# Weight sums of the MLPs' first products on GpSimd, and the inner operands prepared in two pairs instead of one

## The chip, the core and the metric

The kernel runs on one core of a Trainium2 chip. The core has engines that run side by side, each through its own queue in order: TensorE (PE) multiplies matrices, VectorE (DVE) and ScalarE (ACT) work element by element, GpSimd (POOL) does so too, and SyncE (SP) issues the transfers (DMAs) between the chip's large memory and the core's on-chip memory. Engines wait for each other by semaphores. The metric is the device time of one execution in microseconds (us); the kernel before takes 1993.26 us (median of 3 runs, 1992.43 to 1994.49).

## What is computed

A network of two layers on 1024 tokens of width 1024, all in float32. Each layer is a mixer (sliding-window attention in the first, a gated linear recurrence called HGRN2 in the second) and an MLP of width 4096:

```python
def sqrelu_mlp(h, w_up, w_down):
    return jnp.square(jax.nn.relu(h @ w_up)) @ w_down
...
    for layer in range(DEPTH):
        h = rmsnorm(x, mix_norm[layer])
        ...                                   # attention or HGRN2
        x = x + y.astype(x.dtype)
        h = rmsnorm(x, mlp_norm[layer])
        x = x + sqrelu_mlp(h, mlp_w_up[layer], mlp_w_down[layer]).astype(x.dtype)
    return rmsnorm(x, final_norm)
```

The change touches `h @ w_up`, the MLP's first product, and, through a shared helper, some of the HGRN2 projections.

## The kernel before

**Precision.** A float32 matrix is split into a high part (`wh` for a weight, a CAST to a narrower float32 form, on ACT or DVE) and a low part (`wl`, the rest, a subtraction on DVE). `mm3` then makes three matrix multiplications (high by high, high by low, low by high), each 128 x 128 weights by 512 columns.

**Strassen.** Each large product is cut into 2 x 2 blocks and made with seven block products instead of eight (the Strassen-Winograd form). They are numbered 1 to 7; products 1, 2 and 4 take raw weights, products 5, 6, 3 and 7 take sums s1, s2, s4 and s3 of raw weights. The operands on the token side are sums too, made once per MLP.

**The first product of an MLP** (`mlp`, which calls `pair`) runs over 16 pairs m = 0 to 15. `pair` calls `strassen_weights`: it loads four raw weight tiles of 128 x 512 (tag `wr`, 6 buffers), makes the four sums (tag `m`, 7 buffers), and splits the weights of the products to come (tags `wh` and `wl`, 5 buffers each). Seven `product` calls follow, five from pair 4 on, 12 multiplications each, and then the ReLU, the square and the sums of the hidden values (tag `t`, 20 buffers), which are stored for the second product. `two`, which makes the projections of HGRN2, calls `strassen_weights` as well, 12 times.

**Inner blocks.** From pair 4 on, products 2 and 4 of a pair are themselves made with seven smaller products of 256 columns, for two pairs at a time. A generator `inner` does this (12 blocks in each MLP, one in each pair from 3 to 14): it loads two raw tiles, makes four sums of 128 x 256, and issues its products between those of the pair. Their token-side operands are made by a generator `prepare(name)`, once for name 2 and once for name 4: it loads four tiles back from the large memory, makes four differences (each as two halves of 128 x 256 on DVE), splits three of them, and stores seven tiles. Both `prepare` generators are stepped between the products of pair AT = 2; in pair 3 `put_in` loads one of the stored tiles of each, splits it and puts it in place.

**The order.** The instructions are not issued in the order of the code. `Schedule` records them all, with a planner's cost for each engine that may do one, and lists them by a simulated clock: PE work keeps about the order of the code, weights are given a lead (`LEAD`), an operation that two engines can do goes to the one that finishes earlier by these costs. `tt` gives the planner's cost of an elementwise operation of two tensors; with the engine `"any"` it goes to DVE. `only(...)` on a tile tells the planner that just a part of it is touched, so that work on another part needn't be ordered against it. The result is one fixed queue for each engine. Nearly all instructions carry the line of the one call in which they are issued, L374 (in `call`), so the profile's rows are told apart by tile names.

Of the kernel before, what the change touches and what calls it, by code (L numbers as in the profile page):

```python
# [15 lines left out]
ALU = mybir.AluOpType  # L16
# [27 lines left out]
LEVELS = 6  # L44
WARM = 10
INNER = (2, 4)
AT = 2
K_SPANS = ((-1, 3), (2, 6), (5, 8))

# [261 lines left out]
def straight(z):  # L311

    return z.rearrange("p (b a) -> p a b", a=2)


def halves(z):

    return z.rearrange("p (a b) -> p a b", a=2)


class Net:
# [88 lines left out]
        self.s.add({e: ways[e] for e in engines}, [out], [in_])  # L410

    def tt(self, e, out, x, y, alu, n=TH):
        cost = {"DVE": 70 + n * 1.04, "Pool": 147 + n * 2.105}
        engines = ("DVE",) if e == "any" else (e,)
        ways = {e: self.call(self.engine(e).tensor_tensor, out, x, y, alu) + (cost[e],) for e in engines}
        self.s.add(ways, [out], [x, y])
# [101 lines left out]
    def rstd(self, acc, inner=1.0, outer=1.0, n=TH):  # L518
        return self.spread(self.token_rstd(acc, inner, outer, n), n)
# [43 lines left out]
    def finish(self, which, r=None):  # L563
# [36 lines left out]
        for j in range(HK):  # L600
            z = stored(j + HK)
            self.tt("any", z, z, t[j], ALU.subtract)
            x[4].append(self.split(z))
            if r is None and 4 in INNER:
                self.quarters[4].append(self.keep(z))
# [28 lines left out]
    def strassen_weights(self, first, second, done=()):  # L634

        self.s.lead = LEAD
        a = {(i, k): self.raw(src[:, k * TH : k * TH + TH]) for i, src in enumerate((first, second)) for k in range(2)}
        s1, s2, s3, s4 = (self.t(tag="m") for _ in range(4))
        self.tt("any", s1, a[1, 0], a[1, 1], ALU.add)
        self.tt("any", s2, s1, a[0, 0], ALU.subtract)  # L640
        self.tt("any", s3, a[0, 0], a[1, 0], ALU.subtract)
        self.tt("any", s4, a[0, 1], s2, ALU.subtract)
        order = ((1, a[0, 0]), (5, s1), (2, a[0, 1]), (6, s2), (3, s4), (7, s3), (4, a[1, 1]))
        w = {name: self.weight_split(z) for name, z in order if name not in done}
        self.s.lead = 0
        return w

    def prepare(self, name):

        near, far = slice(0, TH // 2), slice(TH // 2, TH)  # L650
        u = [self.t() for _ in range(HK)]
        for z, kept in zip(u, self.quarters[name]):
            self.dma(z, kept, 4 * P * TH)
        yield
        made = self.quarters[name] = {}

        def difference(out, x, y):
            for i in range(2):
                self.tt("any", out[:, i].only(i), x(i), y(i), ALU.subtract, TH // 2)

        def stored(k, t):
            made[k] = [self.keep(z.bitcast(F32)) for z in self.split(t.rearrange("p i c -> p (i c)"), self.t)]

        low, high = (lambda c: lambda i: u[i][:, c]), (lambda c: lambda i: u[2 + i][:, c])
        new = lambda: self.t(F32, (P, 2, TH // 2))
        part = lambda t: lambda i: t[:, i].only(i)
        t1 = new()
        difference(t1, low(far), low(near))
        made[5] = self.keep(t1.rearrange("p i c -> p (i c)"))
        yield  # L670
        t2 = new()
        difference(t2, high(far), part(t1))
        stored(6, t2)
        yield
        t3 = new()
        difference(t3, high(far), low(far))
        stored(7, t3)
        yield
        t4 = new()
        difference(t4, high(near), part(t2))  # L680
        stored(4, t4)
        yield
# [13 lines left out]
    def inner(self, name, m, x, y):  # L696

        near, far, half = slice(0, TH // 2), slice(TH // 2, TH), TH // 2
        row, made = {2: 0, 4: 1}[name], self.quarters[name]
        self.s.lead = LEAD  # L700
        a0, a1 = (self.raw(self.io["up"][self.layer, i + row * (MT // 2)][:, TH:]) for i in (m, m + 1))
        sa, sb = self.t(tag="m"), self.t(tag="m")
        s1, s2, s3, s4 = sa[:, near].only(0), sa[:, far].only(1), sb[:, near].only(0), sb[:, far].only(1)
        self.tt("any", s1, a1[:, near], a1[:, far], ALU.add, half)
        self.tt("any", s2, s1, a0[:, near], ALU.subtract, half)
        self.tt("any", s3, a0[:, near], a1[:, near], ALU.subtract, half)
        self.tt("any", s4, a0[:, far], s2, ALU.subtract, half)
        wide = []
        w = {1: (0, near), 2: (0, far), 5: (1, near), 6: (1, far), 7: (2, near), 3: (2, far), 4: (3, far)}
        self.s.lead = 0  # L710
        banks = [self.psum(), self.psum()]
        main, side, own = banks[0][:, near].only(0), banks[1][:, near].only(0), banks[1][:, far].only(1)

        def product(k, ps, start):
            more = {} if start else {"skip_group_check": True}
            n, cols = w[k]
            self.s.lead = LEAD
            if n == 3:
                hi, lo = (self.tile(tag, BUFS[tag], (P, TH), F32R) for tag in ("wh", "wl"))
                self.copy(hi[:, far], a1[:, far], half, ("ACT", "DVE"), False)  # L720
                self.tt("any", lo[:, far], a1[:, far], hi[:, far].bitcast(F32), ALU.subtract, half)
                wide.append((hi, lo))
            elif n == len(wide):
                wide.append(self.weight_split((a0, sa, sb)[n]))
            if k in made:
                right = [self.t(F32R) for _ in range(2)]
                for z, kept in zip(right, made[k]):
                    self.dma(z.bitcast(F32), kept, 4 * P * TH)
            self.s.lead = 0
            for i in range(2):  # L730
                c = slice(cols.start + i * P, cols.start + i * P + P)
                wh, wl = (z[:, c] for z in wide[n])
                if k in made:
                    xh, xl = (z[:, i * half : (i + 1) * half] for z in right)
                else:
                    at = near if k in (1, 2) else far
                    xh, xl = (z[:, at] for z in x[name][i if k in (1, 5) else 2 + i])
                self.mm3(ps, (wh, wl), (xh, xl), start and i == 0, i == 1, half, slice(0, half), **more)

        y.extend(self.t() for _ in range(2))  # L740
        part = {(i, j): y[i][:, (near, far)[j]].only(j) for i in range(2) for j in range(2)}

        def take(z, bank):
            self.copy(halves(z), straight(bank), half)

        def add(z, bank):
            self.tt("DVE", halves(z), straight(bank), halves(z), ALU.add, half)

        product(1, main, True)
        take(part[0, 0], main)  # L750
        yield
        product(2, own, True)
        add(part[0, 0], own)
        yield
        product(6, main, False)
        take(part[0, 1], main)
        yield
        product(5, side, True)
        take(part[1, 1], side)
        yield  # L760
        product(7, main, False)
        add(part[1, 1], main)
        yield
        product(3, side, False)
        add(part[0, 1], side)
        yield
        product(4, main, False)
        take(part[1, 0], main)
        yield
# [56 lines left out]
    def mlp(self, cut):  # L826

        x = self.mlp_second()
        made, n = {}, MT // 2
        for m in range(n):  # L830
            between, first = [], m - m % 2
            if m == AT:
                between += [self.prepare(name) for name in INNER]
            if m == AT + 1:
                between += [self.put_in(name, x[name]) for name in INNER]
            for name in INNER:
                c = first if name == 4 else first + 2
                if AT < c < n and m % 2 == (name == 2):
                    made[name, c] = []
                    between.append(self.inner(name, c, x, made[name, c]))  # L840
            done = {name: made[name, first][m % 2] if name == 2 else lambda: made[4, first][m % 2] for name in INNER if (name, first) in made}
            if m == n - 2:
                self.r = [self.a() for _ in range(NH)]
                for hf in range(NH):
                    self.copy(self.r[hf], self.spread(self.square[hf]))
            if m == 1 and self.layer == 0:
                self.hgrn_constants()
            self.pair(m, x, done, between)
        yield from self.down(cut)
# [881 lines left out]
```

## Time and profile before

| what | value |
|---|---|
| median of 3 runs | 1993.26 us (1992.43 to 1994.49) |
| the profiled execution, its own time | 1992.46 us |
| its span, first to last instruction | 1990.6 us |
| granted TensorE clock | 0.998 |
| ACT busy | 1108.4 us (56%) |

The profile is of one execution. Busy time is time in which at least one instruction of the engine was under way. A row of a group has: line, engine, operation, output <- inputs (tile names without numbers), shape and type, count | busy us, mean ns of one | idle us of the engine just before. A row of the timeline has: start, length, engine, line, operation, tiles, shape, count of merged instructions, and in brackets the idle time before it and what ended it. A matrix multiplication's end is modelled: it is shown as longer than the distance to the next one's start.

### The profile page before, as it was taken

How to read it: one execution, taken by the hardware profiler on the slowest of the kernel's cores; microseconds unless marked ns; L12 is line 12 of the kernel's file. 1: busy time of each engine (PE TensorE's matmuls, PEld its weight loads, DVE VectorE, ACT ScalarE, POOL GpSimd, SP SyncE). 2: the span in 40 equal slices, each digit the busy share in tenths (PEclk: the TensorE clock that was granted, in tenths of full speed). 3: DMA queues.
4: the chain of work that ended last, by engine and by line, in shares of the span. 5: the costliest groups of instructions: out<-in, count | busy, mean ns of one | idle time of the engine just before them, and what ended most of it. 6: DMA issues, size and time to landing. Idle time of an engine off the chain costs nothing.

```text
span 1990.6 us, 34667 instructions
## 1 busy us (share of the span) xinstructions
PE 1968.2 (99%) x11836; PEld 1723.3 (87%) x11836; DVE 1763.1 (89%) x3557; ACT 1108.4 (56%) x2280; POOL 61.9 (3%) x124
## 2 busy tenths in 40 slices
PE   9999999999999999999999999999999999999998
PEld 8877788899998888888888888888889998888887
DVE  8999899898889878899899999989989888987787
ACT  6567797666664423355455555554766666343352
POOL 4030000000000000000000000000000000000001
PEclk9999999999999999999999999999999999999999
DMA  6211464998889977755412212667599888986752
GB/s 224 90 54 59 127 217 162 308 304 290 285 264 319 330 244 244 242 167 179 140 59 81 75 60 86 206 203 253 185 313 305 285 278 280 317 315 211 239 173 85
DMA packets 232401, 411.04 MB, mean 206 GB/s; under 512 B 25504, under 2 KB 35744, under 8 KB 232224
## 3 DMA queue, kind: packets, MB, share of 16 engines
q1 hardware_dynamic: 231648, 408.30, 62.0%
q8 instruction: 93, 1.52, 0.3%
q14 instruction: 84, 0.69, 0.1%
q10 hardware_dynamic: 576, 0.52, 0.1%
HBM read 305.97 MB, written 102.76 MB: 205 GB/s over the span
## 4 chain that ended last, share of the span: by engine, by line
PE 89%; DVE 6%; issue 2%; ACT 2%; DMA 1%; POOL 0%; POOLq 0%; SPq 0%; DVEq 0%; ACTq 0%
PE q L374 51%; PE p L374 39%; DVE t L374 2%; DVE a L374 1%; DVE wl L374 1%; DVE m L374 1%; ACT t L374 1%; ACT a L374 1%; ACT wh L374 0%; ACT m L374 0%; DMA wr<-in_wo 0%; POOL a L374 0%; DMA wr<-in_up 0%; DMA a<-in_x 0%; DMA d<-t 0%
## 5 line engine op out<-in xcount | busy, mean ns | idle before, releaser
L374 PE MATMUL q<-a,wh 128*128 128x512 f32 x2368 | 708.4, 379 | 1.9 <-ACT t L374 1.6
L374 PE MATMUL p<-a,wh 128*128 128x512 f32 (+1 forms) x2304 | 657.7, 365 | 0.9 <-DVE wh L374 0.8
L374 PEld LDWEIGHTS q<-a,wh 128*128 128x128 f32 x2368 | 438.8, 189 | 59.2 <-ACT t L374 2.4
L374 PEld LDWEIGHTS p<-a,wh 128*128 128x128 f32 x2304 | 421.1, 189 | 55.4 <-issue 1.2
L374 PE MATMUL q<-a,wl 128*128 128x512 f32 x1184 | 448.1, 379 | 0.0
L374 PE MATMUL p<-a,wl 128*128 128x512 f32 (+1 forms) x1152 | 418.4, 364 | 0.0
L374 ACT CAST a<-t 128x512 fp32r<-128x512 f32 (+1 forms) x299 | 178.8, 613 | 216.8 <-PE q L374 126.6
L374 DVE TENSOR_TENSOR t<-t,t 128x512 f32<-128x512 f32 (+3 forms) x424 | 256.0, 628 | 11.6 <-ACT t L374 10.3
L374 PEld LDWEIGHTS q<-a,wl 128*128 128x128 f32 x1184 | 223.9, 189 | 30.3
L374 DVE TENSOR_TENSOR wl<-wr,wh 128x512 fp32r<-128x512 f32 (+1 forms) x352 | 233.8, 667 | 12.2 <-ACT wh L374 4.7
L374 PEld LDWEIGHTS p<-a,wl 128*128 128x128 f32 x1152 | 218.2, 190 | 25.1 <-issue 0.4
L374 DVE TENSOR_TENSOR a<-t,a 128x512 fp32r<-128x512 f32 (+2 forms) x334 | 218.4, 677 | 0.5 <-ACT a L374 0.2
L374 DVE TENSOR_TENSOR wl<-m,wh 128x512 fp32r<-128x512 f32 x296 | 201.6, 684 | 7.6 <-ACT wh L374 4.0
L374 ACT CAST wh<-wr 128x512 fp32r<-128x512 f32 x221 | 131.7, 598 | 136.1 <-PE p L374 46.2
L374 ACT ACTIVATE t<-t 128x512 f32<-128x512 f32 x296 | 183.7, 630 | 35.7 <-DVE t L374 23.5
L374 ACT CAST wh<-m 128x512 fp32r<-128x512 f32 x239 | 147.0, 618 | 89.5 <-PE p L374 38.8
L374 ACT COPY t<-q 128x512 f32<-128x512 f32 (+3 forms) x190 | 105.2, 557 | 63.8 <-PE q L374 59.3
L374 DVE CAST wh<-wr 128x512 fp32r<-128x512 f32 (+1 forms) x131 | 55.0, 419 | 89.2 <-PE q L374 67.2
L374 ACT COPY t<-p 128x256 f32<-128x256 f32 (+1 forms) x157 | 70.5, 452 | 95.4 <-PE p L374 78.0
L374 DVE TENSOR_TENSOR m<-wr,wr 128x512 f32<-128x512 f32 x184 | 118.8, 649 | 3.8 <-DMA wr<-in_down 3.5
L374 PE MATMUL p<-wh,a 128*128 128x512 f32 x352 | 110.9, 385 | 0.0
L374 PEld LDWEIGHTS q<-t,t 128*64 128x64 f32 (+1 forms) x2160 | 95.5, 144 | 14.0 <-issue 6.3
(138 smaller groups left out, 2330.4 us busy)
## 6 DMA issues: line engine op xcount, KB each, us to landing
t<-d SPq DMA_DIRECT2D x428, 256.0 KB, 4.4
d<-t SPq DMA_DIRECT2D x312, 256.0 KB, 4.1
wr<-in_down SPq DMA_DIRECT2D x256, 256.0 KB, 4.2
wr<-in_up SPq DMA_DIRECT2D x176, 256.0 KB, 4.4
a<-d SPq DMA_DIRECT2D x60, 256.0 KB, 4.9
wr<-in_wqkv SPq DMA_DIRECT2D x48, 256.0 KB, 2.9
d<-a SPq DMA_DIRECT2D x48, 256.0 KB, 3.3
wr<-in_win SPq DMA_DIRECT2D x48, 256.0 KB, 2.9
```

The costliest lines, as they stand in the source:

```text
L374: fn(*[place(a) for a in args], **{k: place(v) for k, v in kw.items()})
```

## The change

Three things are done, and two small ones with them.

1. The four sums of raw weights in `strassen_weights` (128 x 512) and in `inner` (128 x 256) go to GpSimd instead of DVE. Over the program these are 176 sums of 128 x 512 (64 in each MLP, 48 in the HGRN2 projections) and 96 of 128 x 256 (48 in each MLP).
2. The planner's cost of such an operation on GpSimd is raised from 147 + 2.105 n to 212 + 3.0 n for n columns. These are the planner's numbers; they decide the order alone.
3. `prepare` for name 2 is stepped in pair 1, that for name 4 in pair 2, instead of both in pair 2.
4. In `prepare`, the table that the inner blocks read is emptied before the first step ends, not after.
5. In `inner`, the three views of the two PSUM banks lose their `only(...)`: for the planner each bank is one thing.

```diff
@@ -44,6 +44,7 @@
 INNER = (2, 4)
+PREPARED = {2: 1, 4: 2}
 AT = 2
@@ -410,7 +411,7 @@
     def tt(self, e, out, x, y, alu, n=TH):
-        cost = {"DVE": 70 + n * 1.04, "Pool": 147 + n * 2.105}
+        cost = {"DVE": 70 + n * 1.04, "Pool": 212 + n * 3.0}
@@ -636,10 +637,10 @@
         s1, s2, s3, s4 = (self.t(tag="m") for _ in range(4))
-        self.tt("any", s1, a[1, 0], a[1, 1], ALU.add)
-        self.tt("any", s2, s1, a[0, 0], ALU.subtract)
-        self.tt("any", s3, a[0, 0], a[1, 0], ALU.subtract)
-        self.tt("any", s4, a[0, 1], s2, ALU.subtract)
+        self.tt("Pool", s1, a[1, 0], a[1, 1], ALU.add)
+        self.tt("Pool", s2, s1, a[0, 0], ALU.subtract)
+        self.tt("Pool", s3, a[0, 0], a[1, 0], ALU.subtract)
+        self.tt("Pool", s4, a[0, 1], s2, ALU.subtract)
@@ -651,8 +652,8 @@
             self.dma(z, kept, 4 * P * TH)
-        yield
         made = self.quarters[name] = {}
+        yield
@@ -701,15 +702,15 @@
-        self.tt("any", s1, a1[:, near], a1[:, far], ALU.add, half)
-        self.tt("any", s2, s1, a0[:, near], ALU.subtract, half)
-        self.tt("any", s3, a0[:, near], a1[:, near], ALU.subtract, half)
-        self.tt("any", s4, a0[:, far], s2, ALU.subtract, half)
+        self.tt("Pool", s1, a1[:, near], a1[:, far], ALU.add, half)
+        self.tt("Pool", s2, s1, a0[:, near], ALU.subtract, half)
+        self.tt("Pool", s3, a0[:, near], a1[:, near], ALU.subtract, half)
+        self.tt("Pool", s4, a0[:, far], s2, ALU.subtract, half)
...
-        main, side, own = banks[0][:, near].only(0), banks[1][:, near].only(0), banks[1][:, far].only(1)
+        main, side, own = banks[0][:, near], banks[1][:, near], banks[1][:, far]
@@ -829,8 +830,7 @@
             between, first = [], m - m % 2
-            if m == AT:
-                between += [self.prepare(name) for name in INNER]
+            between += [self.prepare(name) for name, at in PREPARED.items() if m == at]
```

How the queues change is seen at three places. The first is GpSimd's queue at the start of the first MLP. Before, it holds two small index tables and then nothing until zero tiles of the HGRN2 stage:

```order
L374 TENSOR_SCALAR m_2996<-c_324 128x4
L374 TENSOR_SCALAR m_3155<-c_324 128x4
L374 IOTA t_4204 128x64
L374 IOTA t_4211 128x64
L374 MEMSET t_12172 64x4x64
```

Now the sums of pairs 0 to 3 stand there (the names of the inputs: `wr` is a raw weight, `m` an earlier sum), and those of the first inner block, of 256 columns, behind them:

```order
L375 IOTA t_4205 128x64
L375 IOTA t_4214 128x64
L375 TENSOR_TENSOR m_4217<-wr_4023,wr_4165 128x512
L375 TENSOR_TENSOR m_4235<-wr_4165,wr_4191 128x512
L375 TENSOR_TENSOR m_4254<-m_4235,wr_4023 128x512
L375 TENSOR_TENSOR m_4284<-wr_4044,m_4254 128x512
L375 TENSOR_TENSOR m_4493<-wr_4263,wr_4436 128x512
L375 TENSOR_TENSOR m_4520<-wr_4436,wr_4448 128x512
L375 TENSOR_TENSOR m_4547<-m_4520,wr_4263 128x512
L375 TENSOR_TENSOR m_4568<-wr_4250,m_4547 128x512
L375 TENSOR_TENSOR m_4695<-wr_4655 128x256
```

In a pair the sum s3 (of a raw tile of each row) comes first, then s1, s2 and s4, in a chain. The second place is DVE's queue ahead of the high part of the first inner block's first weight (`wh_4842` before, `wh_4865` now). Before, the work of `prepare` (`t` from `t`) and the inner block's sums (`m`) stand between the weights:

```order
L374 TENSOR_TENSOR t_4766<-t_4543,t_4627 128x256
L374 TENSOR_TENSOR t_4744<-t_4624,t_4666 128x256
L374 TENSOR_TENSOR m_4723<-wr_4512,m_4688 128x256
L374 TENSOR_TENSOR t_4650<-q_4576,t_4650 128x512
L374 TENSOR_TENSOR t_4789<-t_4766,t_4775 128x512
L374 TENSOR_TENSOR t_4797<-t_4744,t_4781 128x512
L374 CAST wh_4809<-wr_4531 128x512
L374 TENSOR_TENSOR wl_4813<-m_4644,wh_4800 128x512
L374 TENSOR_TENSOR wl_4820<-wr_4531,wh_4809 128x512
L374 TENSOR_TENSOR t_4610<-t_4610,t_4755 128x512
L374 TENSOR_TENSOR t_4835<-t_4791,t_4807 128x512
L374 CAST wh_4842<-wr_4512 128x512
```

Now, the same stretch of DVE's queue (`p_4810` is a PSUM tile of the pair):

```order
L375 CAST wh_4794<-m_4568 128x512
L375 TENSOR_TENSOR t_4797<-t_4779,t_4660 128x512
L375 TENSOR_TENSOR wl_4806<-m_4568,wh_4794 128x512
L375 CAST wh_4814<-m_4493 128x512
L375 TENSOR_TENSOR t_4819<-t_4800,t_4797 128x512
L375 TENSOR_TENSOR wl_4828<-m_4493,wh_4814 128x512
L375 TENSOR_TENSOR t_4779<-t_4800,t_4779 128x512
L375 TENSOR_TENSOR t_4839<-t_4790,t_4819 128x512
L375 TENSOR_TENSOR t_4822<-p_4810,t_4822 128x512
L375 TENSOR_TENSOR wl_4852<-wr_4448,wh_4841 128x512
L375 CAST wh_4865<-wr_4572 128x512
L375 TENSOR_TENSOR wl_4874<-wr_4572,wh_4865 128x512
```

The halves of 128 x 256 and the sums are gone from this stretch, and it holds three casts instead of two. The third place is PE at the same point, the last multiplications ahead of the first inner product (`p`, 256 columns). Before:

```order
L374 MATMUL q_4803<-a_3898,wh_4637 128x512
L374 MATMUL q_4803<-a_3848,wl_4653 128x512
L374 MATMUL p_4849<-a_3643,wh_4842 128x256
L374 MATMUL p_4849<-a_3703,wh_4842 128x256
L374 MATMUL p_4852<-a_3683,wh_4842 128x256
L374 MATMUL p_4852<-a_3745,wh_4842 128x256
L374 MATMUL q_4703<-a_3912,wh_4701 128x512
```

Now:

```order
L375 MATMUL q_4843<-a_3848,wl_4685 128x512
L375 MATMUL q_4740<-a_3908,wh_4753 128x512
L375 MATMUL q_4740<-a_3928,wh_4753 128x512
L375 MATMUL q_4740<-a_3908,wl_4762 128x512
L375 MATMUL p_4876<-a_3643,wh_4865 128x256
L375 MATMUL p_4876<-a_3703,wh_4865 128x256
L375 MATMUL p_4879<-a_3683,wh_4865 128x256
L375 MATMUL p_4879<-a_3745,wh_4865 128x256
L375 MATMUL q_4740<-a_3991,wh_4753 128x512
```

Three multiplications of the pair's next product (`q_4740`) have moved ahead of the first inner product; for the rest PE's queue holds the same work in nearly the same order. Ahead of the first MLP, the making of its operands included, no queue differs.

More of the change, by code (lines that the diff above doesn't have):

```diff
@@ L653, in prepare @@
             self.dma(z, kept, 4 * P * TH)
+        made = self.quarters[name] = {}
         yield
-        made = self.quarters[name] = {}
         def difference(out, x, y):
```

## The prediction

> **What bounds the kernel now.** First the page, busy time and the chain that ended last:
>
> ```profile
> PE 1968.2 (99%) x11836; PEld 1723.3 (87%) x11836; DVE 1763.1 (89%) x3557; ACT 1108.4 (56%) x2280; POOL 61.9 (3%) x124
> ...
> PE 89%; DVE 6%; issue 2%; ACT 2%; DMA 1%; POOL 0%; POOLq 0%; SPq 0%; DVEq 0%; ACTq 0%
> ```
>
> PE is busy 99% and carries 89% of the chain. A busy PE needn't be at its peak, so the second view is that of stretches of time (start:end, length, then the engines' busy us with counts, the granted clock, the DMA share, GB/s). The first MLP's first product lies in 300 to 630, and 700 to 800 is plain second-product work:
>
> ```profile
> 300.00:630.00 330.00, 328.03 (x1770) 293.05 (x1770) 296.55 (x583) 214.26 (x407) 0.36 (x2) 1.00 0.82 274
> 700.00:800.00 100.00, 100.00 (x465) 87.58 (x464) 79.76 (x137) 32.84 (x56) 0.00 (x0) 1.00 0.72 238
> ```
>
> 465 multiplications of 512 columns in 100 us are one in 0.215 us; at a granted clock of 1.00 the array takes them without a pause. The change removes no multiplication, so it can win only PE's pauses. In 300 to 630 PE is idle for 330 - 328.0 = 2.0 us, though DVE is busy for 296.6 of 330: a nearly full DVE is hidden behind a full PE. Third view, PE's timeline, for where the pauses are (two stretches, around 370 and around 1470, the same place in the second MLP):
>
> ```profile
> 369.64 0.70 PE L374 MATMUL q<-a,wh 128*128 128x512 f32 x2 [0.30 <-ACT t L374]
> ...
> 376.27 0.71 PE L374 MATMUL p<-a,wh 128*128 128x256 f32 x4 [0.75 <-DVE wh L374]
> 377.69 0.70 PE L374 MATMUL q<-a,wh 128*128 128x512 f32 x2 [0.70 <-ACT t L374]
> ...
> 1469.04 1.13 PE L374 MATMUL q<-a,wh 128*128 128x512 f32 x4 [0.30 <-DVE wh L374]
> ...
> 1480.91 0.70 PE L374 MATMUL q<-a,wh 128*128 128x512 f32 x2 [0.63 <-ACT t L374]
> ```
>
> The bracket understates a pause, because a matmul's end is modelled late: the page shows 0.379 us as the mean of one while its successor starts 0.215 us after it, so some 0.16 us belongs to each. The pauses are 0.46, 0.91, 0.86, 0.46 and 0.79 us: **3.5 us in both MLPs**. All lie at the entry to the inner blocks. The chain of waits of that stretch says why:
>
> ```profile
> 371.34 1.80 DVE t L374 x3
> ...
> 377.69 0.70 PE q L374 x2
> ```
>
> It comes back to PE out of runs of DVE work on `t` tiles: the two preparations of pair 2, together with everything else, overload DVE for one pair.
>
> **The change, part by part.** *The sums.* What they cost on DVE in 300 to 630, from the groups by shape (the first holds 32 of this stage, the rest are of the second product):
>
> ```profile
> L374 DVE TENSOR_TENSOR m<-wr,wr 128x512 f32<-128x512 f32 x39 | 26.4, 683 | 0.6 <-DMA wr<-in_down 0.6
> ...
> L374 DVE TENSOR_TENSOR m<-wr,m 128x256 f32<-128x256 f32 x12 | 5.0, 418 | 0.0
> ```
>
> Back to back, an instruction shown with 0.68 us occupies DVE for 0.60 (below, 347.88 to 348.48) and one of 0.42 for about 0.34. So DVE sheds 64 x 0.60 + 48 x 0.34 = 54.7 us in each first product, 18% of 297. In the HGRN2 projections it sheds 48 x 0.60 = 29 us. On PE's path this is worth only the pauses above. GpSimd has these operations already at the program's end:
>
> ```profile
> L374 POOL TENSOR_TENSOR a<-a,t 128x256 f32<-128x256 f32 x4 | 2.8, 730 | 21.4 <-ACT t L374 21.4
> L374 POOL TENSOR_TENSOR a<-a,t 128x512 f32<-128x512 f32 x2 | 2.5, 1286 | 657.8 <-ACT t L374 657.8
> ```
>
> At these prices a first product gives GpSimd 64 x 1.286 + 48 x 0.73 = 117 us of work. A pair with an inner block takes PE 60 x 0.215 + 42 x 0.112 = 17.6 us; GpSimd's eight sums take 8.1. It isn't the bound. But a sum takes twice as long; is it late? On DVE a pair's four sums stood among other work:
>
> ```profile
> 343.32 0.68 DVE L374 TENSOR_TENSOR m<-wr,wr 128x512 f32<-128x512 f32 x1
> ...
> 347.88 0.68 DVE L374 TENSOR_TENSOR m<-wr,wr 128x512 f32<-128x512 f32 x1
> 348.48 0.68 DVE L374 TENSOR_TENSOR m<-wr,m 128x512 f32<-128x512 f32 x1
> ```
>
> First start to last end is 5.84 us. GpSimd, whose queue holds only sums, needs 4 x 1.286 = 5.1 us. So the chain ends about when it did, unless something holds GpSimd up. SP stands behind the sums too, since a raw tile's buffer is free only after them:
>
> ```profile
> SPq L374 <- DVE m L374: 43.2, 36, 3.0
> ```
>
> SP waited 36 times for a sum between 330 and 640, 43 us in all, with the loads and stores behind it in its queue. With equal chains that stays as it is.
>
> *Do the two engines disturb each other?* The nearest rows are single-input GpSimd operations of 128 columns beside DVE:
>
> ```profile
> 112.96 0.89 POOL L374 TENSOR_SCALAR a<-a 64x128 fp32r<-64x128 f32 x1
> 113.93 0.52 POOL L374 TENSOR_SCALAR a<-a 64x128 fp32r<-64x128 f32 x1
> ...
> 121.81 1.50 POOL L374 TENSOR_SCALAR a<-a 64x128 fp32r<-64x128 f32 x1
> ```
>
> ```profile
> 112.77 0.69 DVE L374 TENSOR_TENSOR wl<-wr,wh 128x512 fp32r<-128x512 f32 x1
> 113.38 0.51 DVE L374 TENSOR_TENSOR a<-a 128x256 f32<-128x256 f32 x1
> 113.91 0.59 DVE L374 TENSOR_TENSOR t<-q,a 64x128 fp32r<-64x128 f32 x2
> ...
> 121.66 0.65 DVE L374 TENSOR_TENSOR wl<-wr,wh 128x512 fp32r<-128x512 f32 x1
> 122.24 0.68 DVE L374 TENSOR_TENSOR m<-m,sm 128x512 f32<-128x512 f32 x1
> ```
>
> They do. Beside DVE work with one input in PSUM (`t<-q,a`) the operation takes 0.52 us; beside one DVE operation with both inputs on chip memory 0.89; beside two of them in a row 1.50. GpSimd waits 0.37 to 0.98 us. DVE loses less: its 256-column operation shows 0.51 instead of 0.42. And in the middle of a longer GpSimd operation DVE runs at its usual 0.43 and 0.68:
>
> ```profile
> 1039.16 1.56 POOL L374 TENSOR_SCALAR a<-t 128x512 f32<-128x512 f32 x1 [25.21 <-ACT t L374]
> ```
>
> ```profile
> 1039.82 0.43 DVE L374 CAST t<-t 128x512 fp32r<-128x512 f32 x1
> 1040.17 0.68 DVE L374 TENSOR_TENSOR wl<-wr,wh 128x512 fp32r<-128x512 f32 x1
> ```
>
> No row has a two-input GpSimd operation beside a two-input DVE one. The ends for it: GpSimd waits 0 to 0.98 us at each sum, DVE loses 0 to a sum's whole 1.286 us. I take 0.37 and 0.09, the nearest rows. Then four sums take 6.6 us, 0.8 more than on DVE, and DVE gives back 112 x 0.09 = 10 of its 54.7 us per MLP. The 0.8 us can show only where a weight is made just ahead of its use, as at the entry to the inner blocks, where the queues still put the cast of the first inner weight right before its product. Once in each MLP that is 1.6 us, of which DVE's relief hides a part: **1.0 us comes back**, between 0 and 1.6.
>
> *The preparation moved.* `prepare` for name 2 takes 8 halves at 0.34 and 3 low parts at 0.60, 4.5 us of DVE, from pair 2 to pair 1, and with it 4 loads and 7 stores of 256 KB on SP's queue. In exchange pairs 0 and 1 lose eight sums, 4.8 us. So pair 1 gets no fuller than it was, and pair 2 loses 6.9 us. The eleven transfers leave the stretch around 370, where the transfers' queue was fullest with both preparations, for one a pair earlier. I count all 3.5 us of pauses as gone; the bounds are none and all.
>
> *The rest.* The raised planner's cost moves nothing by itself; it lets more casts fall to DVE. The dropped `only` makes the inner block's product 5 wait until DVE has read product 2's half of the bank (0.42 us); product 6 and one product of the pair (12 x 0.215 = 2.6 us) lie between, so 0; uncovered, 24 x 0.42 = 10 us. Emptying the table earlier is 0. In HGRN2 the sums leave a stage in which PE waits for DVE mostly in this way (1000 to 1340):
>
> ```profile
> PE q L374 <- DVE t L374: 2.2, 3, 0.8
> ```
>
> Such waits are for the recurrence's own tiles, not for weights; I take 0 of a possible 2.2 us.
>
> **The sum**: the profiled execution took 1992.46 us (span 1990.6 and 1.9 around it); -3.5 + 1.0 = -2.5 gives 1990.0. The median of the runs stands 0.8 above the profiled one, so **1990.8 us**, -0.13%. A measurement of this kernel can tell about 0.2%, 4 us, from no change.
>
> **The rivals.** *A, a larger gain.* All pauses go, nothing comes back, and HGRN2 gives its 2.2 us: 1993.3 - 5.7 = 1987.6. For it: DVE is 297 of 330 busy and any wait for it shrinks. Against: the recurrence's waits are chains, not queueing. Chance 0.24.
>
> *B, late sums, slower.* If GpSimd waits 0.98 us at each sum, four take 9.1 us, 3.2 more than on DVE, and the raw tiles are held as much longer, so SP's loads slip. Place: the two pairs at the entry to the inner blocks, in both MLPs, where PE already paused for weights. Price: four times 3.2, less the 2.5 won: +10, 2004. It decides from a wait of about 0.5 us per sum on, where the delay of 1.3 us outgrows one pause. For it: DVE's long rows of two-input operations, none of which lets GpSimd in at 121.66. Against: with a sixth less work DVE pauses oftener. Chance 0.2.
>
> *C, DVE held up by the sums.* If each sum stopped DVE for its whole length, a first product would ask DVE for 296.6 - 54.7 + 117 = 359 us in 330: +29 each, +58 for both, 2051. It decides from three quarters of a sum's length on, (54.7 + 33.4) / 117. Against it stand DVE's 0.43 and 0.68 at 1040. Chance 0.07. [...]
>
> *D, nothing.* The pauses come from the five buffers of the split weights and stay: 1993.3. Chance 0.07.
>
> **How the numbers follow.** The forecast, 1990.8 with 1989 to 1994, has 0.42; A 0.24, B 0.2, C 0.07, D 0.07. The range runs from A less 2 us, the spread of the three runs, 1985.5, through B to 2004; it leaves out C and a tail at either end. Faster by over 0.2% (below 1989.3): A's 0.24 and 0.02 of the forecast, 0.26. Slower: B's 0.2 less 0.02 for a small one, and C, 0.25. The rest, 0.49, is the same.
>
> **What would show it.** The pauses near 370 and 1470 gone from PE's timeline; DVE some 120 us less busy overall (54.7 x 2 + 29, less what it gives back), GpSimd up by 176 x 1.66 + 96 x 1.1, about 400 us, to 460; DVE's rows of 128 x 512 still at 0.68. GpSimd's sums at 2.2 us or more, with PE waiting for `wl` from `m`, would be B; DVE's idle time before `wl` put down to POOL would be C. The forecast is wrong if PE shows new pauses in 390 to 630, where before there were next to none.

## The result, and the profile after

The changed kernel takes **2165.07 us** (median of 4 runs, 2163.3 to 2170.25) against 1992.85 us (4 runs of before on the same chip): a ratio of 1.0867, 95% interval 1.0847 to 1.0887. The forecast was 1990.8 us with a range up to 2004; the kernel lost 172 us instead.

The page of the changed kernel, its span and busy times:

```profile
span 2162.3 us, 34972 instructions
...
PE 2025.5 (94%) x11836; PEld 1755.2 (81%) x11836; DVE 1857.8 (86%) x3445; ACT 1031.6 (48%) x2120; POOL 417.3 (19%) x396
```

Two things stand out. PE has 137 us without work (2162.3 - 2025.5), where it had 22. And DVE, which lost 272 sums and gained 160 casts from ACT (3557 to 3445 instructions in all, ACT's 2280 to 2120), is busy 95 us *longer* (1857.8 against 1763.1). Fewer instructions in more time means that they take longer on average. The groups by shape say which; in the stretch from 300 us to the end, kernel before first (count, then busy us and mean ns of one, then idle time ahead):

```profile
L374 DVE TENSOR_TENSOR t<-t,t 128x512 f32<-128x512 f32 x286 | 189.5, 683 | 8.6 <-ACT t L374 7.9
L374 DVE CAST wh<-m 128x512 fp32r<-128x512 f32 x57 | 24.2, 425 | 20.5 <-PE q L374 16.0 <-PE p L374 3.9
L374 DVE TENSOR_TENSOR t<-q,t 128x512 f32<-128x512 f32 x60 | 40.9, 683 | 0.0
```

```profile
L375 DVE TENSOR_TENSOR t<-t,t 128x512 f32<-128x512 f32 x285 | 248.5, 894 | 4.9 <-ACT t L375 4.2
L375 DVE CAST wh<-m 128x512 fp32r<-128x512 f32 x175 | 104.2, 595 | 57.3 <-PE q L375 41.8 <-PE p L375 14.9
L375 DVE TENSOR_TENSOR t<-q,t 128x512 f32<-128x512 f32 x60 | 40.7, 680 | 0.0
```

The operation with both inputs in on-chip memory (`t<-t,t`) went from 683 to 894 ns, the cast from 425 to 595; the one with an input in PSUM (`t<-q,t`) stays where it was, 683 and 680. Now one pair of the first MLP, where the same picture comes back every 23.3 us. PE's timeline of the changed kernel (start, length, then the operation; in brackets the idle time ahead and what ended it):

```profile
484.20 0.38 PE L375 MATMUL q<-a,wl 128*128 128x512 f32 x1
488.38 0.80 PE L375 MATMUL p<-a,wh 128*128 128x256 f32 x2 [3.80 <-ACT wh L375]
...
511.68 0.49 PE L375 MATMUL p<-a,wh 128*128 128x256 f32 x2 [3.80 <-ACT wh L375]
```

PE stands still for 3.97 us (488.38 - 484.20 - 0.215, a matmul's pace) until ACT has cast a weight's high part. ACT's own queue shows why the cast was late:

```profile
486.52 1.29 ACT L375 ACTIVATE t<-t 128x512 f32<-128x512 f32 x2 [3.37 <-DVE t L375]
487.72 0.60 ACT L375 CAST wh<-wr 128x512 fp32r<-128x512 f32 x1
```

The cast (`wh<-wr`, which needs a raw weight alone and starts once ACT is free) stood behind two activations of the pair's hidden values, and those waited 3.37 us for a `t` of DVE. What DVE and GpSimd did meanwhile, in their timelines:

```profile
480.05 1.65 DVE L375 TENSOR_TENSOR t<-t,t 128x512 f32<-128x512 f32 x1
...
481.95 1.43 DVE L375 TENSOR_TENSOR wl<-m,wh 128x512 fp32r<-128x512 f32 x1
483.30 1.52 DVE L375 CAST wh<-m 128x512 fp32r<-128x512 f32 x1
484.74 1.75 DVE L375 TENSOR_TENSOR t<-t,t 128x512 f32<-128x512 f32 x1
486.41 0.68 DVE L375 TENSOR_TENSOR wl<-m,wh 128x512 fp32r<-128x512 f32 x1
```

```profile
479.87 2.96 POOL L375 TENSOR_TENSOR m<-wr,wr 128x512 f32<-128x512 f32 x2 [2.90 <-DVE wl L375]
482.91 1.62 POOL L375 TENSOR_TENSOR m<-m,wr 128x512 f32<-128x512 f32 x1
484.61 1.33 POOL L375 TENSOR_TENSOR m<-wr,m 128x512 f32<-128x512 f32 x1
```

The two engines take turns. GpSimd's sums end at 482.83, 484.53 and 485.94; DVE's operations end 0.55, 0.29 and 0.55 us after those, at 483.38, 484.82 and 486.49, and once the sums are over DVE is back at 0.68. These three and the `t<-t,t` at 480.05 take 6.35 us; at 0.68 and 0.43 they would take 2.47. The 3.9 us between are as long as PE's pause.

This is so in the whole trace. From 300 us on, 132 two-input operations and casts of 128 x 512 take DVE longer than 1.1 us, and every one of them ends 0.2 to 0.65 us after an instruction of GpSimd. Of the `t<-t,t`, 72 overlap with a sum for more than 0.2 us and take 1.52 us on average; the others take 0.68. Twelve `t<-q,t` overlap as well and still take 0.68.

A second loss follows it, in the view of stretches (start:end, length, busy us and counts of PE, PEld, DVE, ACT and POOL, granted clock, DMA share, GB/s):

```profile
484.40:488.40 4.00, 0.20 (x2) 0.02 (x1) 4.00 (x6) 1.77 (x3) 1.46 (x2) 0.98 0.39 125
488.40:491.60 3.20, 3.20 (x10) 2.75 (x11) 1.89 (x4) 0.63 (x1) 0.00 (x0) 0.50 1.02 378
491.60:507.70 16.10, 16.10 (x94) 14.38 (x93) 12.56 (x20) 6.51 (x13) 7.52 (x7) 1.00 0.65 206
```

After the pause PE runs 3.2 us at a granted clock of 0.50, with 0.43 us from one multiplication of 512 columns to the next (488.96 to 489.39) instead of 0.215, which costs another 1.6 us. A pair of 17.6 us of work with 3.97 + 1.6 makes 23.2, and the pairs are 23.3 apart. Of the 24 pairs with an inner block 20 show such a pause, of 3.75 to 3.98 us, 79 us in all. The half clock does not follow each of them. The trace's records of the clock come in steps of 3.41 us; behind 16 of the 20 pauses there is a step at 0.50 (once two), behind four there is none, as here, after the pause that ends at 466.18:

```profile
466.20:469.40 3.20, 3.20 (x21) 2.99 (x22) 3.03 (x6) 1.47 (x4) 0.00 (x0) 1.00 1.02 380
```

By these records PE works at half clock for 95 us of the execution, 54 of them behind the 20 pauses, and half of that time is lost. So the 20 pauses and their half clock make 79 + 27 = 106 of the 172 us. One longer pause, of 6.4 and 6.1 us, stands at the start of each MLP, behind its first eight sums; half clock elsewhere costs some 20 us, and the rest is shorter pauses. In the view of PE's waits (us in total, times, longest), the first row holds 18 of the 20 pauses, and the longest wait of the second is such a start:

```profile
PE p L375 <- ACT wh L375: 69.0, 19, 3.8
PE q L375 <- DVE t L375: 19.1, 8, 6.1
```

### The profile page after: what moved, and what is told of

Its sections match the earlier page's. It is cut to its first block, busy times and chain, and to the rows that moved or that the text cites. A ratio compares the mean times of both kernels' runs of the same rounds, so it can differ in the third digit from the quotient of the medians.

```text
span 2162.3 us, 34972 instructions
## 1 busy us (share of the span) xinstructions
PE 2025.5 (94%) x11836; PEld 1755.2 (81%) x11836; DVE 1857.8 (86%) x3445; ACT 1031.6 (48%) x2120; POOL 417.3 (19%) x396
## 3 DMA queue, kind: packets, MB, share of 16 engines
q8 instruction: 93, 1.52, 0.3%
## 5 line engine op out<-in xcount | busy, mean ns | idle before, releaser
L375 PE MATMUL p<-a,wh 128*128 128x512 f32 (+1 forms) x2304 | 674.6, 374 | 82.1 <-ACT wh L375 69.0
L375 PE MATMUL q<-a,wh 128*128 128x512 f32 x2368 | 723.7, 388 | 7.9 <-ACT t L375 6.7
L375 POOL TENSOR_TENSOR m<-wr,wr 128x512 f32<-128x512 f32 (+1 forms) x112 | 168.5, 1515 | 864.6 <-DMA wr<-in_win 401.9
L375 DVE TENSOR_TENSOR t<-t,t 128x512 f32<-128x512 f32 (+3 forms) x424 | 319.9, 781 | 7.8 <-ACT t L375 6.6
L375 DVE TENSOR_TENSOR wl<-m,wh 128x512 fp32r<-128x512 f32 x296 | 230.1, 778 | 19.2 <-PE q L375 10.1
L375 ACT CAST wh<-wr 128x512 fp32r<-128x512 f32 x187 | 114.5, 616 | 117.4 <-PE p L375 50.5
L375 DVE CAST wh<-wr 128x512 fp32r<-128x512 f32 (+1 forms) x165 | 75.2, 456 | 110.4 <-PE q L375 88.8
L375 DVE CAST wh<-m 128x512 fp32r<-128x512 f32 x175 | 104.2, 595 | 57.3 <-PE q L375 41.8
L375 ACT CAST wh<-m 128x512 fp32r<-128x512 f32 x121 | 74.8, 618 | 81.1 <-PE p L375 40.2
L375 PE MATMUL q<-t,t 128*64 128x32 f32 (+2 forms) x2160 | 105.4, 230 | 8.5 <-ACT t L375 4.3
```

The source lines that it names most:

```text
L375: fn(*[place(a) for a in args], **{k: place(v) for k, v in kw.items()})
```

## The experiments

Two theories stand against each other, and the expectations tell them by their mechanism. **Shut out**: a GpSimd sum, which reads two on-chip inputs, and a DVE operation with two on-chip inputs (or a cast) exclude each other for an instruction's whole length. The expectations call it 'port', a name only: no run shows what the two engines share. **Late** (rival B of the prediction): the sums come too late from a slow engine, and whoever needs them or the raw tiles' buffers waits. Beside them, the other parts of the change could be the cause.

| kernel | median us | ratio to before (95%) | against before |
|---|---|---|---|
| changed kernel | 2165.07 | 1.0867 (1.0847 to 1.0887) | +172 |
| sums back on DVE | 1992.57 | 0.9999 (0.9990 to 1.0007) | 0 |
| sums only | 2166.55 | 1.0871 (1.0852 to 1.0890) | +174 |
| old planner's cost | 2173.95 | 1.0903 (1.0888 to 1.0918) | +181 |
| write only | 2013.71 | 1.0098 (1.0084 to 1.0112) | +21 |
| one input | 2033.50 | 1.0199 (1.0180 to 1.0218) | +41 |
| beside | 2090.71 | 1.0486 (1.0471 to 1.0502) | +98 |
| pieces | 2090.08 | 1.0488 (1.0471 to 1.0506) | +97 |
| HGRN2 sums only | 2007.18 | 1.0068 (1.0053 to 1.0083) | +15 |
| pair sums only | 2121.52 | 1.0641 (1.0618 to 1.0664) | +128 |
| inner sums only | 2021.08 | 1.0141 (1.0127 to 1.0155) | +28 |
| one sum of a pair | 2012.43 | 1.0097 (1.0083 to 1.0111) | +19 |
| preparation a pair earlier still | 2001.69 | 1.0041 (1.0027 to 1.0055) | +8.5 |

(The last column is against the median of the runs of before that were made beside each kernel's, 1992.6 to 1993.2.)

### Which part of the change

*Sums back on DVE*: the changed kernel with its eight sums as they were; preparation, `only` and table stay changed.

```diff
-        self.tt("Pool", s1, a[1, 0], a[1, 1], ALU.add)
+        self.tt("any", s1, a[1, 0], a[1, 1], ALU.add)
...
```

> The changed kernel with its sums back on DVE: the preparation in two pairs, the emptied table and the dropped part marks stay. Theory 'port' (GpSimd's two-input sums and DVE's operations with two on-chip inputs or casts shut each other out, DVE falls behind in bursts): 1990 us, within 3, since no sums are left on GpSimd. Theory 'late' (a sum takes 1.3 to 1.7 us instead of 0.6 and raw tiles are freed later): also 1990. Theory 'order' (the moved preparation or the planner's new order is bad): above 2050.

*Sums only*: before with the eight `"any"` made `"Pool"` and the raised cost, nothing else.

```diff
-        cost = {"DVE": 70 + n * 1.04, "Pool": 147 + n * 2.105}
+        cost = {"DVE": 70 + n * 1.04, "Pool": 212 + n * 3.0}
...
-        self.tt("any", s1, a[1, 0], a[1, 1], ALU.add)
+        self.tt("Pool", s1, a[1, 0], a[1, 1], ALU.add)
...
```

> The kernel before with only the sums on GpSimd and the raised planner's cost; both preparations in pair 2. 'port' and 'late': 2150 to 2180, all of the loss. If the moved preparation had a part in the loss: below 2120.

*Old planner's cost*: the changed kernel with the cost line of before.

```diff
-        cost = {"DVE": 70 + n * 1.04, "Pool": 212 + n * 3.0}
+        cost = {"DVE": 70 + n * 1.04, "Pool": 147 + n * 2.105}
```

> The changed kernel with the planner's old cost of a GpSimd sum (147 + 2.105 n). 'port' and 'late': 2150 to 2180. 'order' (the cost makes the planner place casts and loads badly): below 2060.

Measured: 1992.57, 2166.55 and 2173.95 us. The sums are the whole loss, and the rest of the change neither costs nor wins anything that can be told from nothing. The raised cost is worth some 9 us once the sums are on GpSimd, and doesn't touch the mechanism.

### Lateness or the shared inputs

*Write only*: the changed kernel, each sum done on GpSimd in 2 columns, with the others filled with a constant twice, so that GpSimd is about as long busy (407.3 us of the execution against 417.3), in the same order, with the same waits.

```diff
+    def filled(self, out, x, y, alu, n=TH):
...
+            g.tensor_tensor(place(out[:, :2]), place(x[:, :2]), place(y[:, :2]), alu)
+            for _ in range(2):
+                g.memset(place(out[:, 2:]), 0.01)
...
-        self.tt("Pool", s1, a[1, 0], a[1, 1], ALU.add)
+        self.filled(s1, a[1, 0], a[1, 1], ALU.add)
...
```

> The changed kernel, same planner's cost and order, but each sum on GpSimd is a sum of 2 columns and then two fills of the rest with a constant: GpSimd waits for the same tiles and is busy about as long (1.2 to 1.4 us), yet reads almost nothing. The weights of products 5, 6, 3 and 7 are left out in this way. 'port': DVE's 128x512 rows back at 0.68 us, the pauses of 4 us gone, 1990 to 2010. 'late': the fills end as late as sums, 2120 to 2170.

Measured: 2013.71, a little above 2010, and 151 us below the changed kernel. The same stretch of both, 300 to 630; first the changed kernel, then write only:

```profile
300.00:630.00 330.00, 277.63 (x1380) 240.38 (x1379) 275.81 (x433) 141.43 (x263) 136.69 (x106) 0.93 0.64 210
```

```profile
300.00:630.00 330.00, 323.71 (x1714) 283.38 (x1713) 267.76 (x524) 173.78 (x327) 135.51 (x338) 0.99 0.78 261
```

GpSimd is busy 136.7 us in the first and 135.5 in the second, and yet PE does 1714 matmuls instead of 1380 in the same time. DVE's groups of write only, in the stretch from 300 us on:

```profile
L375 DVE TENSOR_TENSOR t<-t,t 128x512 f32<-128x512 f32 x285 | 188.1, 682 | 5.4 <-ACT t L375 4.5
L375 DVE CAST wh<-m 128x512 fp32r<-128x512 f32 x175 | 89.8, 513 | 41.4 <-PE q L375 28.9 <-PE p L375 11.9
```

The two-input operation is back at 682; the cast, at 513, is still longer than the 425 of before. The page has DVE busy for 1712.0 us in the same 3445 instructions, 146 less than in the changed kernel: that is what GpSimd's reads put on DVE. Of the 21 us that are still lost, some 9 stand at the old place. At the point of a pair where PE paused 4 us, a cast of DVE now takes 0.87 us instead of 0.43 beside the fills, and PE waits about 0.36 us for the same cast of ACT as before, 18 times (0.52 with the 0.16 that the view hides at each pause). In one pair:

```profile
488.73 0.87 DVE L375 CAST wh<-m 128x512 fp32r<-128x512 f32 x1
```

```profile
492.08 0.49 PE L375 MATMUL p<-a,wh 128*128 128x256 f32 x2 [0.35 <-ACT wh L375]
```

*One input*: the same, with one copy of one input in place of the fills.

```diff
+            g.tensor_tensor(place(out[:, :2]), place(x[:, :2]), place(y[:, :2]), alu)
+            g.tensor_scalar(place(out[:, 2:]), place(x[:, 2:]), 1.0, None, ALU.mult)
```

> The changed kernel, same order, each GpSimd sum replaced by a sum of 2 columns and a copy of the rest from one input (a tensor by a scalar, 1.5 us in the trace of before); the weights of products 5, 6, 3 and 7 are left out in this way. If any reading by GpSimd shuts out DVE's two-input operations for its length: 2120 to 2180. If only two-input GpSimd operations do, as the rows at 1039 of the kernel before seemed to allow: 2000 to 2040, near the run with fills.

Measured: 2033.5. DVE's group and GpSimd's, from 300 us on:

```profile
L375 DVE TENSOR_TENSOR t<-t,t 128x512 f32<-128x512 f32 x285 | 201.6, 729 | 5.0 <-ACT t L375 4.2
...
L424 POOL TENSOR_SCALAR m<-wr 128x510 f32<-128x510 f32 x132 | 226.7, 1717 | 0.0
```

A copy holds GpSimd for 1.72 us, no less than a sum, and DVE loses 46 ns on average (729 against 683) where beside the sums it lost 211. So it isn't the length of GpSimd's instruction that hurts: of the 172 us, 21 remain with no reads, 41 with one input, and the step from the copy to the sum brings the other 131. (The copy is also another operation than the sum; the number of inputs was not changed alone.)

*Beside*: before, its sums on DVE, and after each of them GpSimd adds a scratch tile to itself. Nobody waits for its result. (The scratch tile takes one of the 58 `a` buffers.)

```diff
+    def beside(self, out, x, y, alu, n=TH):
+        self.tt("any", out, x, y, alu, n)
...
+            g.tensor_tensor(place(z[:, :2]), place(out[:, :2]), place(out[:, :2]), ALU.add)
+            g.tensor_tensor(place(z[:, 2:n]), place(z[:, 2:n]), place(z[:, 2:n]), ALU.add)
...
-        self.tt("any", s1, a[1, 0], a[1, 1], ALU.add)
+        self.beside(s1, a[1, 0], a[1, 1], ALU.add)
...
```

> The kernel before, sums on DVE as they were (one buffer of tag a fewer), and after each sum GpSimd adds a scratch tile to itself, two reads of 510 or 254 columns, 272 such additions; nobody waits for their result. 'port': DVE is held up although it makes its own sums and none is late; it carries 110 us more than in the changed kernel, so 2170 to 2260. 'late' (the cause is that the sums end later and hold the raw tiles): 1993 to 2000.

Measured: 2090.71. Work that nobody waits for costs 98 us, and no wait of DVE or PE for GpSimd shows in the trace; under the theory of lateness it should have been free. But it is less than expected of the shut-out. Its group from 300 us on and its stretch 300 to 630:

```profile
L376 DVE TENSOR_TENSOR t<-t,t 128x512 f32<-128x512 f32 x285 | 209.0, 752 | 6.5 <-ACT t L376 6.1
```

```profile
300.00:630.00 330.00, 298.81 (x1567) 258.77 (x1566) 307.82 (x515) 190.50 (x363) 173.36 (x226) 0.98 0.70 233
```

DVE is lengthened less per operation (752 against 894), and the clock is at 0.98 where it was 0.93. The pauses are more and shorter, as its two largest rows of PE's waits show:

```profile
PE p L376 <- DVE t L376: 20.3, 22, 1.7
PE p L376 <- DVE wl L376: 18.8, 21, 1.6
```

*Pieces*: the changed kernel, each sum cut into pieces of 128 columns; same reads, same results, shorter instructions.

```diff
+    def pieces(self, out, x, y, alu, n=TH):
...
+            for c in range(0, n, P):
+                self.nc.gpsimd.tensor_tensor(*(place(z[:, c : c + P]) for z in (out, x, y)), alu)
```

> The changed kernel with each GpSimd sum cut into pieces of 128 columns. If an instruction holds the port for its whole length, a DVE operation waits for one piece of about 0.4 us and not for a sum of 1.3: rows of 128x512 on DVE near 1.1 us at most, and 2050 to 2130; the pieces' own fixed cost makes the sums longer. If the two share the port by cycles, the cut changes nothing for DVE and the longer sums make it 2165 to 2220.

Measured: 2090.08. In 300 to 630:

```profile
300.00:630.00 330.00, 297.04 (x1559) 254.55 (x1559) 280.70 (x474) 155.39 (x292) 251.26 (x354) 0.98 0.71 233
```

GpSimd is busy 251 us of 330 there, nearly twice as long, and the kernel is 75 us *faster* than with whole sums. From 300 us on no two-input operation or cast of 128 x 512 on DVE exceeds 0.98 us, where it was up to 1.79; on average `t<-t,t` takes 812 ns there instead of 894, and the cast 538 instead of 595. A lateness would have grown; a hold that lasts one instruction shrinks with the instruction.

### How the loss is spread

Each kernel is before with the raised cost and a part of the sums on GpSimd. *HGRN2 sums only* (48 of 128 x 512):

```diff
-    def strassen_weights(self, first, second, done=()):
+    def strassen_weights(self, first, second, done=(), e="any"):
...
-        self.tt("any", s1, a[1, 0], a[1, 1], ALU.add)
+        self.tt(e, s1, a[1, 0], a[1, 1], ALU.add)
...
-        w = self.strassen_weights(*sources)
+        w = self.strassen_weights(*sources, e="Pool")
```

> The kernel before with only the 48 sums of the HGRN2 projections on GpSimd. 'port': the same DVE operations are stretched there, but weights are ready longer ahead of their use, so little is left on PE: 1998 to 2012. If that stage gains from a lighter DVE as the rival A of the prediction had it: 1988 to 1991.

*Pair sums only* (128 of 128 x 512; the same function, `"Pool"` passed by `pair` instead):

> The kernel before with only the 128 sums of 128x512 of the two MLPs on GpSimd. 'port': each of the four in a row holds DVE up for about 1.1 us at the place where the pair's hidden values are made; most of the loss, 2090 to 2150.

*Inner sums only* (96 of 128 x 256; the four lines in `inner` alone):

> The kernel before with only the 96 sums of 128x256 of the inner blocks on GpSimd. 'port': half as long, four in a row; 2000 to 2030. If the loss goes by GpSimd's time alone (35 of 117 us in each MLP): 30% of the MLPs' loss of about 160 us, 2040.

*One sum of a pair* (32; only s3, the sum off the chain):

```diff
-        self.tt("any", s3, a[0, 0], a[1, 0], ALU.subtract)
+        self.tt(e, s3, a[0, 0], a[1, 0], ALU.subtract)
```

> The kernel before with one sum of each pair, s3, on GpSimd: 32 sums, none of them in a row with another. 'port': DVE loses 0.5 net per pair and has that much slack: 1992 to 2002. If a lighter DVE can win anything at all here, this is where: 1989 to 1991.

Measured: +14.6, +128.3, +27.9 and +19.2 us. The first three add up to 170.8, close to the 174 of sums only, so the parts hardly help or hurt each other. Per sum that is 0.30 us in HGRN2, 1.00 in the pairs, 0.29 in the inner blocks, and 0.60 for a single s3. The last was a miss; its DVE timeline shows how little is needed (its sum runs from 472.41 to 473.69):

```profile
472.19 0.75 DVE L374 TENSOR_TENSOR t<-p,t 128x256 f32<-128x256 f32 x2
472.86 1.38 DVE L374 TENSOR_TENSOR t<-t,t 128x512 f32<-128x512 f32 x1
474.16 0.68 DVE L374 TENSOR_TENSOR wl<-m,wh 128x512 fp32r<-128x512 f32 x1
```

The operation that meets the sum gets 0.70 us longer, though DVE was spared a sum of 0.60. DVE's account is nearly even, and the kernel still loses 0.6 us for each. In this stretch the delay falls on an operation that ACT waits for (1.45 us before its next activation, at 474.27); that the saving falls where DVE was not waited for is a reading, not measured.

### The preparation

*Preparation a pair earlier still*: the kernel with the sums back on DVE, with

```diff
-PREPARED = {2: 1, 4: 2}
+PREPARED = {2: 0, 4: 1}
```

> As the run with the sums back on DVE, and the two preparations one pair earlier still, in pairs 0 and 1. If the pauses follow the preparation (DVE is full in every one of the first pairs, so that its work is only paid elsewhere): the same as that run, 1990 to 1994, with PE's pauses of 0.5 to 1.2 us now near 320 to 345. If they belong to the entry to the inner blocks and only need time: 1988 to 1990, pauses gone.

Measured: 2001.69, slower than either theory had it. PE's pauses around the entry in the first MLP, first with the sums back on DVE, then with the earlier preparation:

```profile
341.81 0.48 PE L375 MATMUL q<-a,wl 128*128 128x512 f32 x1 [0.49 <-DVE wl L375]
357.86 0.70 PE L375 MATMUL q<-a,wh 128*128 128x512 f32 x2 [0.68 <-DVE wh L375]
359.60 0.70 PE L375 MATMUL q<-a,wh 128*128 128x512 f32 x2 [1.04 <-ACT t L375]
```

```profile
340.11 0.70 PE L375 MATMUL q<-a,wh 128*128 128x512 f32 x2 [1.28 <-ACT wh L375]
343.57 0.80 PE L375 MATMUL q<-a,wl 128*128 128x512 f32 x1 [2.77 <-DVE wl L375]
...
365.15 0.70 PE L375 MATMUL q<-a,wh 128*128 128x512 f32 x2 [1.23 <-DVE wh L375]
```

The pauses of before at 370 and 377 have moved to 342 to 360, and then in part to 340 to 344, with some left at 365. Counted as the prediction counts them, in both MLPs, they are 3.5 us before, 3.7 with the sums back on DVE and some 9 with the earlier preparation (2.08 us at 1431.10 among them): with the sums on DVE they don't shrink, and at the earliest place they grow.

With the sums off DVE it is otherwise. Write only has the moved preparation too, and a DVE that neither makes the sums nor is held up by reads. The entry in the first MLP (length and PE's busy time are the second and third number), in before, with the sums back on DVE, and in write only, where no pause over 0.2 us stands between 317 and 418:

```profile
360.00:390.00 30.00, 28.24 (x147) 24.48 (x146) 25.91 (x54) 18.46 (x35) 0.00 (x0) 1.00 0.93 312
```

```profile
330.00:360.00 30.00, 27.79 (x127) 23.39 (x126) 29.85 (x86) 19.86 (x36) 0.00 (x0) 1.00 0.71 244
```

```profile
330.00:360.00 30.00, 30.00 (x140) 26.10 (x139) 29.16 (x85) 18.07 (x32) 13.83 (x22) 1.00 0.71 250
360.00:390.00 30.00, 30.00 (x152) 26.36 (x152) 22.26 (x45) 13.97 (x25) 7.14 (x23) 1.00 0.90 298
```

## Why the prediction was wrong

**What bounds the kernel.** That PE's pauses were all that could be won is not contradicted: no kernel here won anything. But a nearly full DVE behind a full PE, which the prediction named, cuts both ways: what lengthened DVE's operations showed on PE almost at once, in the pair at 484 as 3.97 us without work behind 3.9 us lost on DVE.

**The step that failed: "I take 0.37 and 0.09, the nearest rows".** It took the price of a sum for DVE from GpSimd operations with *one* input on 128 columns, and the row at 1039.16, taken as DVE running freely in the middle of a longer GpSimd operation, was one-input too. The one-input kernel shows that this reading was true of one-input operations (46 ns lost on average) and not of sums (211 ns). The prediction had the upper end, a sum's whole length, among its bounds, said that no row showed the case, and still gave it 0.07. In place of 0.09 us the 272 sums put 146 us on DVE (changed kernel against write only), 0.54 each; where the forecast had 1.0 us coming back on PE's path, the sums cost 174 (sums only). GpSimd's side of the step, 0.37, was near.

**Rival C had the mechanism, with the wrong size.** An operation of DVE that meets a sum is held up until the sum ends, as at 484.74: 1.75 us for an operation of 0.68. What GpSimd runs beside it makes the difference: `t<-t,t` takes 894 ns on average beside the sums, 729 beside copies of one input and 682 beside fills, which read nothing (casts beside fills 513, against 425). C's price, +58, was worked out from DVE's load over the whole stage (359 of 330) with a threshold at three quarters of a sum's length. The real price is three times that, though DVE lost only about half of the sums' length (146 us; alone they would take 176 x 1.286 + 96 x 0.73 = 296): below C's threshold, so by C's own account nothing should have been lost. The timelines of the pair show why the average misleads: the four sums come in one burst on top of the operations that make the pair's hidden values, DVE falls 3.9 us behind there, and ACT's queue hands this on to the next weight. It doesn't help that DVE has time to spare elsewhere in the pair. Nor did the sign named for C come, idle time of DVE put down to POOL: the trace has none, for the hold lies inside DVE's own rows, as their greater length.

**The clock was in no term.** PE works at half clock for 95 us, which costs some 47; before has 2 us of it, at its end. Before had no pause near 4 us, its longest wait of PE being 1.9, and its clock stood at 1.00 in the MLPs. In the changed kernel half clock comes in steps of 3.41 us, and behind 16 of the 20 pauses of about 4 us. The length of a pause doesn't settle it: four of the 20 leave the clock at 1.00, and a pause of 1.82 us which ends at 1184.89 is followed by a step at 0.50, from 1187.99 on.

**Rival B is not the cause.** Sums do wait on GpSimd, as its groups in the changed kernel show against 1286 ns without DVE's load:

```profile
L375 POOL TENSOR_TENSOR m<-wr,wr 128x512 f32<-128x512 f32 x88 | 148.7, 1702 | 864.6 <-DMA wr<-in_win 401.9 <-DVE wl L375 187.5 <-DMA wr<-in_up 144.1
L375 POOL TENSOR_TENSOR m<-m,wr 128x512 f32<-128x512 f32 x44 | 68.1, 1548 | 16.2 <-issue 8.6 <-PE q L375 4.0 <-POOL m L375 0.7
L375 POOL TENSOR_TENSOR m<-wr,m 128x512 f32<-128x512 f32 x44 | 61.2, 1390 | 34.6 <-DVE wl L375 23.2 <-issue 4.3 <-DVE sm L375 3.8
```

That is 0.42, 0.26 and 0.10 us each, near the 0.37 that the forecast took. But write only has nearly as busy a GpSimd and the same waits with 21 us lost, beside loses 98 us without one late sum, and pieces, with GpSimd's sums longer still, lose less.

**DVE some 120 us less busy: wrong twice.** In write only, where the two-input operations are free of it, DVE is only 51 us less busy than before, for one thing because 160 casts came over from ACT, which the prediction costed at nothing; the reads then add 146. (It put such casts down to the raised cost; with the old cost the counts are almost the same, 3443 instructions on DVE.) GpSimd's 460 us was near (417).

**The preparation: "I count all 3.5 us of pauses as gone".** This step held on its own premise. The argument that pair 1 "gets no fuller" rested on the eight sums leaving DVE. Where they leave it and no reads hold DVE up, in write only, the pauses at the entry are gone; where they stay on DVE, the pauses only move and the ratio is 0.9999. In the changed kernel what was won there can't be seen beside what the sums cost.

**Right at nothing**: `only` and the table, both still changed in the kernel with 0.9999. The raised cost, put at nothing too, wins 9 us once the sums are on GpSimd. **HGRN2**, taken as 0 of a possible 2.2 us, lost 14.6, a third of the price per sum; the hold shows there too (in the changed kernel a `wl<-m,wh` at 1060.01 takes 1.79 us beside a sum).

**Open.** Beside loses 98 us and the changed kernel 172. The half clock (95 us of PE's work against 22) covers some 36 of these 74; what share the burst of four waited-for sums and the other order of casts have in the rest was not separated. Nor were the some 12 us of write only that are left beside its 18 short pauses (casts moved to DVE, and sums that come later, among the candidates). No version beat before.

## What to carry to other kernels

A price for two engines side by side is only as good as the likeness of its row: number of inputs and length must match, or the bound on the bad side deserves a real chance. Price it at the place where the operations meet, not on a stage's average load, and follow the delay through the queue of the engine that waits. An engine that is 19% busy is no free one if its instructions stop an engine that is 89% busy.

## What the runs showed of the hardware

- A two-input sum on GpSimd and a cast, or an operation with two on-chip inputs, on DVE run one after the other (132 operations of over 1.1 us, each ending 0.2 to 0.65 us behind a GpSimd instruction), and cutting the sums into pieces of 128 columns made the kernel 75 us faster though GpSimd was busy nearly twice as long. One-input copies of the same width hold DVE less: `t<-t,t` takes 729 ns on average beside them, 894 beside the sums and 683 in before.
- GpSimd was held up in turn. At the start of the first MLP two sums, 2.57 us without DVE's load, take 7.01 us while DVE's queue runs without a pause (and the first two of the next pairs 8.06 at 334.13 and 7.18 at 356.73). The sums after these then hold DVE up, and PE waits 6.13 us behind the start's eight:

```profile
297.98 7.01 POOL L375 TENSOR_TENSOR m<-wr,wr 128x512 f32<-128x512 f32 x2 [53.11 <-DVE wl L375]
```

```profile
322.36 1.44 PE L375 MATMUL q<-c,t 128*128 128x1 f32 x6 [6.13 <-DVE t L375]
```

- A pause of about 4 us on PE costs some 5.6 where half clock follows, 16 of 20 times. The other four lie across the border of two of the 3.41 us steps, with PE busy for 37 to 47% of each. In beside, whose two largest rows of PE's waits have none over 1.7 us, the clock in 300 to 630 was 0.98, where the changed kernel had 0.93.
